# Seven block products in place of eight for half of an output projection, with half of z between them, on one Trainium2 core

## The chip, the cores and the metric

The kernel runs on one core of a Trainium2 chip. The metric is device time in microseconds, the median of several runs. Beside it one execution was profiled: its span runs from the first to the last instruction. The runs of the kernel before read 955.54, 956.37 and 956.94 us; the profiled span is 953.9 us. The profile gives no time around the span.

## The reference

One decoder layer on 512 tokens of width 1024, in float32:

```python
proj = x @ w_in
z, xbc, dt_raw, q, k, v, g = _split_cols(proj, IN_SIZES)
...                       # SSD scan of x|B|C gives y; retention of q, k, v gives yr
u = (y.reshape(bsz, seqlen, SSD_INNER) * jax.nn.silu(z.astype(f32)))    # then RMS norm -> y_ssd
yr = yr * gn_w.astype(f32) + gn_b.astype(f32)
y_ret = jax.nn.silu(g.astype(f32)) * yr
y_mix = jnp.concatenate([y_ssd, y_ret], axis=-1).astype(x.dtype)
return y_mix @ w_out      # 2048 x 1024; the lower 1024 rows are the retention half
```

After it come a layer norm, cross attention into 256 memory tokens, a second norm, a gated feed-forward of width 2752 and a third norm.

## The kernel before

Every dense product is done in three matmuls. A float32 operand is split into a part h (a cast to fp32r) and a rest l, and `mm3` (L156) adds h·h, h·l and l·h in a PSUM bank. Weights come as one stream of 157 groups of 128x1024 (`Stream`, L111): a DMA on SP's queue into one of three raw slots, a cast on ScalarE to `wh`, a subtraction on VectorE to `wl` (on GpSimd for the groups in `POOL_L`). Three groups are prepared ahead of the one in use, in rings of four.

TensorE's order is the order in which the code is written (`pin`, L96). The other engines' order comes from a list scheduler that takes, of what it thinks ready, what stands first in the code. A dense product is a generator. `feat` (L161) makes 128 features by 512 tokens out of one weight group, in four steps of six matmuls; `tok` (L172) makes four token tiles by 512 columns out of several groups, four steps of six matmuls a group, with the evacuation `done(t, b)` in the last group. `weave` (L198) runs a chain of dependent work and takes as many dense steps between its pieces as the chain yields.

The stages, in order:

- q, k, v (L267 to L366); the retention core (`retention`, L374) in four chunks of 128 tokens, woven into the x|B|C projection with 2 + 2 + 6 + 1 steps a chunk; its normalised outputs are transposed into `YT` after the six;
- the SSD (`ssd`, L520), four chunks woven into the eight gate products (one per retention head, `gate`, L608) and the first half of z (`z_gate`, L622). A gated head is split into `yret`, one cast and one subtraction of 128x512 each. In an SSD chunk `seg` (L541) makes decay factors on ScalarE, multiplies them on VectorE (L550), and `diag` (L553) uses them in the first products on them some steps later;
- the second half of z alone (L638); the z gate runs over ScalarE, VectorE and GpSimd (L623 to L632);
- four residual loads into `acc` on GpSimd's queue, kept in program order (L642);
- the retention half of the output projection: two `tok` products (column halves) of eight groups, added to `acc` by `into_acc` (L645). Woven into it, `ssd_out` (L669) transposes the SSD's output tile by tile after 4, 3, 3 and 3 steps and splits it;
- the SSD half (L716 to L727), the first norm, keys and values of the memory, attention, second norm, feed-forward, third norm.

`norm_t` (L703) transposes a normed token tile into `xT`, two splits of 128x512 a tile. Tiles lie in several sets of buffers: `s` (20), `acc` (4), `row` (2) and `x` (4 of double size).

## Time and profile before

| what | us |
| --- | --- |
| median of three runs (955.54 to 956.94) | 956.37 |
| span of the profiled execution | 953.9 |
| TensorE busy | 944.3 |
| VectorE busy | 563.6 |
| ScalarE busy | 340.9 |
| GpSimd busy | 140.0 |

Busy time is the time in which an engine works on an instruction; waiting for semaphores is not in it. The ends of matmuls are modelled and overlap, so 382 ns of one matmul is not the pace of many: the pace is read from a run of matmuls in the chain of waits. The mean granted TensorE clock was 0.998 of full speed.

### The profile page before, as it was taken

How to read it: one execution, taken by the hardware profiler on the slowest of the kernel's cores; microseconds unless marked ns; L12 is line 12 of the kernel's file. 1: busy time of each engine (PE TensorE's matmuls, PEld its weight loads, DVE VectorE, ACT ScalarE, POOL GpSimd, SP SyncE). 2: the span in 40 equal slices, each digit the busy share in tenths (PEclk: the TensorE clock that was granted, in tenths of full speed). 3: DMA queues.
4: the chain of work that ended last, by engine and by line, in shares of the span. 5: the costliest groups of instructions: out<-in, count | busy, mean ns of one | idle time of the engine just before them, and what ended most of it. 6: DMA issues, size and time to landing. Idle time of an engine off the chain costs nothing.

```text
span 953.9 us, 11550 instructions
## 1 busy us (share of the span) xinstructions
PE 944.3 (99%) x4607; PEld 776.5 (81%) x4607; DVE 563.6 (59%) x847; ACT 340.9 (36%) x487; POOL 140.0 (15%) x150
## 2 busy tenths in 40 slices
PE   9999999999999999999999999999999999999996
PEld 6788877788777888889888888988888888888874
DVE  5652566687765463448645668766535566336577
ACT  4122333345443431223533413544323443224420
POOL 1330110014252530065000006000000000000003
PEclk9999999999999999999999999999999999999999
DMA  8233211222211262425621112432322323323202
GB/s 296 87 115 103 67 45 67 67 89 67 67 45 67 89 221 88 154 89 176 221 88 47 67 66 89 136 108 88 98 101 89 111 89 95 103 89 110 89 22 89
DMA packets 26981, 95.24 MB, mean 100 GB/s; under 512 B 3120, under 2 KB 3632, under 8 KB 26928
## 3 DMA queue, kind: packets, MB, share of 16 engines
q1 hardware_dynamic: 25056, 88.09, 27.7%
q0 software_dynamic: 1728, 6.29, 1.9%
q8 instruction: 36, 0.59, 0.3%
q14 instruction: 17, 0.14, 0.1%
q10 hardware_dynamic: 144, 0.13, 0.0%
HBM read 92.41 MB, written 2.10 MB: 99 GB/s over the span
## 4 chain that ended last, share of the span: by engine, by line
PE 97%; DVE 1%; DMA 1%; SPq 0%; issue 0%; ACT 0%; DVEq 0%
PE b L104 95%; PE b L108 3%; DMA raw<-in_wst 1%; DVE acc L699 0%; DVE acc L692 0%; DVE x L153 0%; SPq L221 0%; DVE wl L128 0%; DVE acc L857 0%; DVE st L687 0%; ACT wh L126 0%; SPq L124 0%; DVEq L1073 0%; DVE st L688 0%
## 5 line engine op out<-in xcount | busy, mean ns | idle before, releaser
L104 PE MATMUL b<-x,wh 128*128 128x512 f32 (+1 forms) x1200 | 359.1, 382 | 0.5 <-DVE x L153 0.5
L128 DVE TENSOR_TENSOR wl<-raw,wh 128x1024 fp32r<-128x1024 f32 (+1 forms) x146 | 179.9, 1234 | 225.9 <-ACT wh L126 225.3
L126 ACT CAST wh<-raw 128x1024 fp32r<-128x1024 f32 (+1 forms) x157 | 164.8, 1050 | 311.5 <-PE b L104 275.1
L104 PEld LDWEIGHTS b<-x,wh 128*128 128x128 f32 x1200 | 218.2, 188 | 45.0 <-issue 4.2
L104 PE MATMUL b<-x,wl 128*128 128x512 f32 (+1 forms) x600 | 227.1, 378 | 0.0
L104 PE MATMUL b<-wh,s 128*128 128x512 f32 (+2 forms) x680 | 214.1, 391 | 0.0
L104 PE MATMUL b<-wh,x 128*128 128x512 f32 x512 | 163.2, 395 | 0.0
L104 PEld LDWEIGHTS b<-wh,s 128*128 128x128 f32 (+1 forms) x680 | 127.3, 188 | 30.7 <-issue 5.1
L104 PE MATMUL b<-wl,s 128*128 128x512 f32 (+1 forms) x340 | 131.5, 387 | 0.0
L104 PEld LDWEIGHTS b<-x,wl 128*128 128x128 f32 x600 | 112.9, 188 | 21.3
L104 PEld LDWEIGHTS b<-wh,x 128*128 128x128 f32 x512 | 96.0, 188 | 23.6 <-issue 2.2
L104 PE MATMUL b<-wl,x 128*128 128x512 f32 x256 | 99.9, 390 | 0.7 <-DVE wl L128 0.7
L104 PEld LDWEIGHTS b<-wl,s 128*128 128x128 f32 x340 | 63.9, 188 | 12.2
L257 POOL TENSOR_TENSOR st<-st,epst 128x1 f32<-128x1 f32 (+1 forms) x16 | 3.1, 192 | 479.6 <-DVE st L688 479.2
L894 DVE SCALAR_TENSOR_TENSOR t<-b,pr,t 128x511 f32<-128x511 f32 x86 | 64.1, 746 | 1.4
L104 PEld LDWEIGHTS b<-wl,x 128*128 128x128 f32 x256 | 48.1, 188 | 11.4 <-DVE wl L128 1.1
L128 POOL TENSOR_TENSOR wl<-raw,wh 128x1024 fp32r<-128x1024 f32 x12 | 34.8, 2916 | 68.5 <-ACT wh L126 68.5
L892 ACT ACTIVATE t<-b,cw,pr 128x512 f32<-128x512 f32 x43 | 33.3, 775 | 0.0
L908 ACT CAST s<-t 128x512 fp32r<-128x512 f32 (+1 forms) x22 | 13.6, 620 | 54.3 <-DVE t L906 54.3
L897 ACT ACTIVATE t<-t 128x512 f32<-128x512 f32 x21 | 13.3, 632 | 42.2 <-DVE t L895 42.2
L649 DVE TENSOR_TENSOR acc<-acc,b 128x512 f32<-128x512 f32 x24 | 15.8, 678 | 17.9 <-PE b L104 17.9
L104 PE MATMUL b<-s,wh 128*128 128x256 f32 x128 | 23.4, 285 | 0.0
(166 smaller groups left out, 856.3 us busy)
## 6 DMA issues: line engine op xcount, KB each, us to landing
raw<-in_wst SPq DMA_DIRECT2D x156, 512.0 KB, 3.3
row<-in_rows POOLq DMA_DIRECT2D x7, 512.0 KB, 6.2
acc<-in_xn POOLq DMA_DIRECT2D x4, 512.0 KB, 6.4
s<-in_xt SPq DMA_DIRECT2D x3, 512.0 KB, 7.7
out_y<-acc SPq DMA_DIRECT2D x3, 512.0 KB, 2.6
raw<-in_memt SPq DMA_DIRECT2D x2, 512.0 KB, 3.3
raw<-in_wst SPq DMA_DIRECT2D x2, 256.0 KB, 3.3
s<-in_xt SPq DMA_DIRECT2D x2, 256.0 KB, 4.3
```

The source lines that it names most:

```text
L104: pin(nc.tensor.matmul(o, lhsT=lhsT, rhs=rhs, start=start, stop=stop))
L108: pin(nc.tensor.transpose(o, i, ident[:p, :p]))
L126: copy(out=h[:, c], in_=r[:, c])
L128: sub_l(out=l[:, c], in0=r[:, c], in1=f(h[:, c]), op=sub)
L257: gtt(out=o, in0=v, in1=epst[:, :n], op=add)
L649: tt(out=a, in0=a, in1=b, op=add)
L892: nc.scalar.activation(out=c, in_=u, func=AF.Identity, bias=cw[0][:, i:i + 1], scale=ffp[:, i, 2:3])
L894: stt(out=c[:, d:], in0=u[:, :T - d], scalar=ffp[:, i, 2 - d:3 - d], in1=c[:, d:], op0=mult, op1=add)
L897: nc.scalar.activation(out=c, in_=c, func=AF.Silu)
L908: nc.scalar.copy(out=hd[:n, 0, :], in_=ca[:n, :])
```

## The change

The retention half of the output projection, 512 tokens x 1024 by 1024 x 1024, is cut in quarters on both sides and done in seven block products (Winograd's form of Strassen's scheme). `Sides` makes the sums of the left side in place in `YT`: with heads 2 and 3 it splits the first quarter, with heads 6 and 7 the second, and forms four combinations of 128x512 each time; the other five operands are split by `make` up to two products ahead. `Quarter` makes those of the right side: eight raw weight blocks are loaded four items further ahead than the ring, each load on SP's queue held until TensorE has reached that place in the program; item T2 has three combinations of 128x1024 on VectorE, T3 one, for each of two row blocks. Each product has two items of 12 matmuls. Products that share a PSUM bank pair are added there (`start` False), and after each product its sum is evacuated into `acc`.

The second half of z is no longer done alone: one of its four groups follows each of the first four products. The residual loads now stand in the program before it. The SSD's transposes wait for 51 steps. A retention chunk has 2 + 2 + 4 steps, and its outputs are transposed in the next chunk, after the scores. All large tiles come from one set of 37 buffers; `xT` is eight tiles instead of four, and `norm_t` makes four splits of 128x256. The descriptor area of DMAs issued by GpSimd is set to 4096 bytes. The same code can treat v and the down projection so, which `SEVEN` leaves off.

```diff
-NS = 20
-# columns of the constant array
+NS = 37
+SEVEN = ("ret",)
+RET_MIX = (1, 1, 1, 1, 0, 0, 0)
+AHEAD = 4
...
-    def slot(tag, shape, dt=F32, bufs=4):
-        return act.tile(shape, dt, tag=tag, name=nm(tag), bufs=bufs)
     def big(shape, dt=F32):
-        return slot("s", shape, dt, NS)
+        return act.tile(shape, dt, tag="s", name=nm("s"), bufs=NS)
...
+    class Quarters:
+        ORDER = ("11", "21", "T2", "T1", "T3", "22", "T4")
+        def __init__(self, n):
+            self.n, self.r = n, {}
+        def items(self):
+            return [[Quarter(self, what, k) for k in range(2)] for what in self.ORDER]
+    class Quarter:
+        PLACE = {"110": 0, "111": 1, "210": 2, "211": 3, "120": 4, "220": 5, "121": 6, "221": 7}
+        def __init__(self, of, what, k):
+            self.of, self.what, self.k = of, what, str(k)
+        def load(self):
+            for q in {"11": ("11",), "21": ("21",), "T2": ("12", "22")}.get(self.what, ()):
+                t = big([P, 1024])
+                d = nc.sync.dma_start(out=t, in_=wst[self.of.n + self.PLACE[q + self.k]])
+                tc.add_manual_dep(d.ins, last_pe[0].ins.name,
+                                  mybir.DependencyInfo(mybir.DependencyClass.Sync, mybir.DependencyReason.DATA),
+                                  reason="not before its time")
+                self.of.r[q + self.k] = t
+        def split(self):
+            r, k = self.of.r, self.k
+            b11, b12, b21, b22 = [r.get(q + k) for q in ("11", "12", "21", "22")]
+            src = {"11": b11, "21": b21, "T1": b11, "T3": b12, "22": b22, "T4": b21}.get(self.what)
+            if self.what == "T2":
+                src = raw_slot()
+                tt(out=b11, in0=b12, in1=b11, op=sub)
+                tt(out=src, in0=b22, in1=b11, op=sub)
+                tt(out=b21, in0=b21, in1=src, op=sub)
+            elif self.what == "T3":
+                tt(out=b12, in0=b22, in1=b12, op=sub)
+            h, l = pair()
+            nc.scalar.copy(out=h, in_=src)
+            tt(out=l, in0=src, in1=f(h), op=sub)
+            return h, l
...
+        def push(self, *args):
+            self.q.append(self.plan[self.n].split(*args))
             self.n += 1
         def get(self, n):
-            while self.n < self.total and self.n <= self.i + RING - 1:
+            while self.m < len(self.plan) and self.m <= self.i + RING - 1 + AHEAD:
+                self.plan[self.m].load()
+                self.m += 1
...
+    def mixed(products, others, after):
+        out, others = [], list(others)
+        for p, n in zip(products, after):
+            out += p
+            out += others[:n]
+            others = others[n:]
+        return out + others
+    plan = groups(0, 8)
+    plan += mixed(Quarters(8).items(), groups(16, 4), V_MIX) + groups(20, 8) if "v" in SEVEN else groups(8, 20)
+    plan += groups(28, 12)
+    plan += mixed(Quarters(44).items(), groups(40, 4), RET_MIX) if "ret" in SEVEN else groups(40, 12)
...
+    def seven(side, done):
+        bk = {}
+        order = ((1, "11", "u", True), (2, "12", "b", True), (6, "S2", "u", False), (5, "S1", "c", True),
+                 (7, "S3", "u", False), (3, "S4", "c", False), (4, "22", "u", False))
+        def product(i):
+            m, a, where, start = order[i]
+            if start:
+                bk[where] = [bank() for _ in range(2)]
+            for n in range(i, min(i + 3, 7)):
+                side.make(order[n][1])
+            for kp in range(2):
+                wh, wl = W.get(2)
+                for t in range(2):
+                    for j in range(2):
+                        k = 2 * kp + j
+                        mm3(bk[where][t], side(a, k, t), (wh[:, j, :], wl[:, j, :]), start and k == 0, k == 3, not start)
+                    if kp == 1:
+                        done(m, t, bk[where][t])
+                    yield
+        return [product(i) for i in range(7)]
+    def behind(products, others, after):
+        for p, n in zip(products, after):
+            yield from p
+            for _ in range(n):
+                yield from next(others)
+    GOES = {1: (0, 0, True), 2: (0, 0, False), 6: (0, 1, True), 5: (2, 1, True), 7: (2, 1, False),
+            3: (0, 1, False), 4: (2, 0, True)}
+    class Sides:
+        def __init__(self, raws, have=None):
+            self.raws, self.got = raws, dict(have or {})
+        def pair(self, name):
+            if name not in self.got:
+                self.got[name] = big([P, 4, 256], F32R), big([P, 4, 256], F32R)
+            return self.got[name]
+        def split(self, name, p, src):
+            h, l = self.pair(name)
+            c = slice(2 * p, 2 * p + 2)
+            nc.scalar.copy(out=h[:, c, :], in_=src)
+            tt(out=l[:, c, :], in0=src, in1=f(h[:, c, :]), op=sub)
+        def view(self, i, j, p):
+            return self.raws[2 * j + p][:, :, 256 * i:256 * i + 256]
+        def ready(self, p):
+            if p < 2:
+                if p == 0:
+                    self.s1 = None
+                    self.own = "11" not in self.got
+                if self.own:
+                    self.split("11", p, self.view(0, 0, p))
+                return
+            p -= 2
+            if self.s1 is None:
+                self.s1 = big([P, 4, 256])
+            s1 = self.s1[:, 2 * p:2 * p + 2, :]
+            a11, a12, a21, a22 = [self.view(i, j, p) for i in range(2) for j in range(2)]
+            if self.own:
+                self.split("12", p, a12)
+            tt(out=s1, in0=a21, in1=a22, op=add)
+            tt(out=a21, in0=a11, in1=a21, op=sub)
+            tt(out=a11, in0=s1, in1=a11, op=sub)
+            tt(out=a12, in0=a12, in1=a11, op=sub)
+        def make(self, name):
+            if name in self.got:
+                return
+            for p in range(2):
+                self.split(name, p, {"S1": lambda: self.s1[:, 2 * p:2 * p + 2, :], "S2": lambda: self.view(0, 0, p),
+                                     "S3": lambda: self.view(1, 0, p), "S4": lambda: self.view(0, 1, p),
+                                     "22": lambda: self.view(1, 1, p)}[name]())
+        def __call__(self, a, k, t):
+            g = self.got[a]
+            if callable(g):
+                return g(k, t)
+            return g[0][:, k, t * P:(t + 1) * P], g[1][:, k, t * P:(t + 1) * P]
...
+            if c > 0:
+                yn_transposes(c - 1, yn)
             yield 2
...
-            yield 6
...
-            yield 1
...
+            yield 4
+        yn_transposes(NT - 1, yn)
...
+            if "ret" in SEVEN:
+                stt(out=y, in0=sg, scalar=0.5, in1=y, op0=mult, op1=mult)
+                if j in (2, 3, 6, 7):
+                    ret_side.ready(j // 4 * 2 + j % 2)
+                return
...
+    ret_side = Sides([YT[0], YT[2], YT[1], YT[3]])
...
-    drain(tok(x_lhs, all8, NT, z_gate(1)))
-    acc = [slot("acc", [P, 1024], F32) for _ in range(NT)]
+    z_rest = tok(x_lhs, all8, NT, z_gate(1))
+    if "ret" not in SEVEN:
+        drain(z_rest)
+    acc = [big([P, 1024]) for _ in range(NT)]
...
+    def acc_quarter(scale=None):
+        def done(m, t, b):
+            t0, n, first = GOES[m]
+            into_acc(n, scale if first else None)(t0 + t, b)
+        return done
...
-        yield 4
+        yield 51 if "ret" in SEVEN else 4
         for t in range(NT):
-            ys = slot("x", [P, 2, 8, P], F32R)
-            to_features(X[t], lambda g: ys[:, 0, 4 * g:4 * g + 4, :], lambda g: ys[:, 1, 4 * g:4 * g + 4, :])
-            yssd.append(ys)
-            yield 3
-    dense = seq(*[tok(tok2(yret), all8, NT, into_acc(n, ALPHA)) for n in range(2)])
+            yssd.append((big([P, 8, P], F32R), big([P, 8, P], F32R)))
+            to_features(X[t], split_into(*yssd[t]))
+            yield 4 if "ret" in SEVEN else 3
+    if "ret" in SEVEN:
+        dense = behind(seven(ret_side, acc_quarter(ALPHA)), pieces(z_rest, NT), RET_MIX)
+    else:
+        dense = seq(*[tok(tok2(yret), all8, NT, into_acc(n, ALPHA)) for n in range(2)])
...
     def norm_t(t):
-        to_features(acc[t], lambda g: xT[g][:, :, t * P:(t + 1) * P], lambda g: xT[2 + g][:, :, t * P:(t + 1) * P])
+        def put(g, b):
+            for i in range(2):
+                h, l = [x[:, :, t * P:(t + 1) * P] for x in xT[2 * g + i]]
+                split_ps(b[:, 2 * i:2 * i + 2, :], h, l)
+        to_features(acc[t], put)
...
+    heads = np.concatenate([np.arange(P) + 1024 + P * h for h in (0, 2, 1, 3, 4, 6, 5, 7)])
+    g.append(_quarters(wo, heads, every) if "ret" in SEVEN else _tok(wo, slice(1024, 2048), every))
...
-    nc = bacc.Bacc("TRN2", target_bir_lowering=False, num_devices=1)
+    nc = bacc.Bacc("TRN2", target_bir_lowering=False, num_devices=1, dynamic_dma_scratch_size=4096)
```

## Rows read from the trace of the kernel before

**Rows 1.** The page: busy us (share) xinstructions of each engine.

```profile
PE 944.3 (99%) x4607; PEld 776.5 (81%) x4607; DVE 563.6 (59%) x847; ACT 340.9 (36%) x487; POOL 140.0 (15%) x150
```

**Rows 2.** The waits of TensorE: line waited for, us in total, times, longest.

```profile
PE b L104 <- DVE wl L128: 0.7, 1, 0.7
PE b L104 <- DVE x L153: 0.5, 1, 0.5
```

**Rows 3.** Chain in order of time, 300 to 430 us: start, us, what.

```profile
336.96 0.87 PE b L108 x8
337.83 4.10 PE b L104 x18
341.93 0.87 PE b L108 x8
342.81 4.13 PE b L104 x18
```

**Rows 4.** Windows: stretch, length, busy us (x) per engine, clock, DMA share, GB/s.

```profile
197.00:217.00 20.00, 20.00 (x102) 16.78 (x101) 16.85 (x27) 9.97 (x18) 0.00 (x0) 1.00 0.32 105
309.40:378.90 69.50, 69.50 (x324) 57.87 (x323) 33.64 (x42) 25.19 (x43) 22.69 (x37) 1.00 0.40 136
105.00:199.00 94.00, 94.00 (x535) 75.75 (x534) 61.19 (x153) 33.88 (x56) 12.66 (x20) 1.00 0.20 65
```

**Rows 5.** VectorE by line, 309.4 to 378.9 us: busy, mean ns, idle before.

```profile
L128 DVE TENSOR_TENSOR wl<-raw,wh 128x1024 fp32r<-128x1024 f32 x12 | 14.6, 1221 | 18.8 <-ACT wh L126 18.8
L632 DVE SCALAR_TENSOR_TENSOR s<-s,st,row 128x512 f32<-128x512 f32 x8 | 6.1, 763 | 11.4 <-POOL st L631 11.4
L651 DVE SCALAR_TENSOR_TENSOR acc<-acc,b 128x512 f32<-128x512 f32 x8 | 5.4, 684 | 2.2 <-PE b L104 2.2
```

**Rows 6.** Five lines' own views: duration ns min/median/max, first and last start.

```profile
L512 DVE TENSOR_TENSOR acc<-s,dt x4: 1216/1220/2308, 216.0 to 278.1; 128x1024 f32<-128x1024 f32 x4
...
L537 DVE TENSOR_TENSOR t<-b,cs x4: 411/424/424, 219.0 to 289.7; 128x256 f32<-128x256 f32 x4
...
L126 ACT CAST wh<-raw x157: 620/1055/1072, 5.6 to 921.2; 128x1024 fp32r<-128x1024 f32 x156, 128x512 fp32r<-128x512 f32 x1
...
L616 ACT CAST s<-t x8: 602/620/621, 215.8 to 276.7; 128x512 fp32r<-128x512 f32 x8
...
L617 DVE TENSOR_TENSOR s<-t,s x8: 677/688/1026, 217.2 to 277.5; 128x512 fp32r<-128x512 f32 x8
```

**Rows 7.** VectorE in order of time, 255 to 290 us.

```profile
266.64 1.19 DVE L614 SCALAR_TENSOR_TENSOR t<-t,s 128x512 f32<-128x512 f32 x1
...
269.68 1.96 DVE L550 TENSOR_TENSOR t<-t,t 128x512 f32<-128x512 f32 x2 [0.32 <-ACT t L549]
```

**Rows 8.** TensorE in order of time, 262 to 292 us.

```profile
271.19 1.08 PE L104 MATMUL b<-acc,t 128*128 128x64 f32 x8
```

**Rows 9.** The page's DMA issues: KB each, us to landing.

```profile
raw<-in_wst SPq DMA_DIRECT2D x156, 512.0 KB, 3.3
```

**Rows 10.** GpSimd in order of time, 280 to 350 us.

```profile
320.50 0.22 POOL L631 TENSOR_SCALAR st<-st 128x1 f32<-128x1 f32 x1
...
341.81 0.22 POOL L631 TENSOR_SCALAR st<-st 128x1 f32<-128x1 f32 x1
342.02 2.20 POOL L642 DMA_DIRECT2D acc<-in_xn  x4
```

**Rows 11.** The view of L642, the residual loads.

```profile
DMA to landing us min/median/max: 3.6/6.4/10.0
```

**Rows 12.** The view of L626, the z gate's multiplication.

```profile
L626 POOL TENSOR_TENSOR s<-s,t x8: 1280/1293/2203, 307.8 to 337.0; 128x512 f32<-128x512 f32 x8
```

More of the change, by code (lines that the diff above doesn't have):

```diff
@@ L189, in drain, with pieces @@
+    def pieces(gen, n):
+        while True:
+            yield islice(gen, n)
     def drain(*gens):
@@ L282, in rotary, with v_quarter @@
         return done
+    def v_quarter(m, t, b):
+        t0, n, first = GOES[m]
+        v = V[t0 + t][:, n * 512:(n + 1) * 512]
+        if first:
+            nc.scalar.copy(out=v, in_=b)
+        else:
+            tt(out=v, in0=v, in1=b, op=add)
     def v_done(n):
@@ L372, in tile_layer, with yn_transposes @@
     YT = [big([P, 2, T]) for _ in range(4)]
+    def yn_transposes(c, yn):
+        for g in range(2):
+            b = bank()
+            for j in range(4):
+                transpose(b[:, j * P:(j + 1) * P], yn[g][:, j * P:(j + 1) * P])
+            for j in range(2):
+                nc.scalar.copy(out=YT[2 * g + j][:, :, c * P:(c + 1) * P],
+                               in_=b[:, 256 * j:256 * j + 256].rearrange("p (j t) -> p j t", j=2))
     def retention():
+        yn = None
         for c in range(NT):
@@ L486, in xbc @@
     def xbc():
-        for g in range(2):
-            yield from feat(xk, T, conv_silu(8 + g, BT[:, g, :]))
-        for g in range(2):
-            yield from feat(xk, T, conv_silu(10 + g, CT[:, g, :]))
+        if not BC:
+            for tile_ in bc_tiles():
+                yield from tile_
         b_transposes()
@@ L752, in v_mem @@
         return done
-    xT = [slot("x", [P, 4, T], F32R) for _ in range(4)]
+    xT = new_x()
     def first_norm():
@@ L860, in tile_layer @@
     gs = [W.get(2) for _ in range(4)]
-    xT = [slot("x", [P, 4, T], F32R) for _ in range(4)]
+    xT = new_x()
     for t in range(NT):
@@ L932, in tile_layer @@
     drain(hg)
[L933 to L939 removed]
+    up = (feat(xk, T, ff_done(i)) for i in range(4, NFF))
+    if "down" in SEVEN:
+        drain(*islice(up, 14))
+        drain(behind(seven(hid_side[0], acc_quarter(ALPHA)), up, UP_MIX[0]))
+        drain(*islice(up, 2))
+        drain(behind(seven(hid_side[1], acc_quarter()), up, UP_MIX[1]))
+        drain(*up)
+    else:
+        for n in range(2):
+            drain(*islice(up, 16 if n else 12))
+            for m in range(2):
+                drain(tok(tok2(hid), range(8 * n, 8 * n + 8), NT, into_acc(m, None if n else ALPHA)))
+        drain(*up)
+    for n in range(2):
+        drain(tok(tok2(hid), [16, 17], NT, into_acc(n)))
     gs = [W.get(2) for _ in range(4)]
```

187 lines of the change are left out of this document (114 added, 73 removed).

## The prediction

> **What bounds the kernel now.** I read the busy table first. TensorE is busy 944.3 of 953.9 us, VectorE 563.6 [rows 1]. The list of TensorE's waits comes next: behind its matmuls stand two waits of 0.7 and 0.5 us and nothing else after the start [rows 2]. So the kernel is one queue of matmuls, and an edit changes the time in two ways only: it takes matmuls out of the queue, or it makes the queue wait. The chain of waits gives the price of a matmul: 18 products of 512 columns in 4.13 us, 0.229 us each [rows 3].
>
> The profiled span is 953.9 us; the three runs of before read 955.54 to 956.94. I take 2.5 us around the span, so a span of X goes with X + 2.5, and a change of the span is carried to the median of 956.37 unchanged.
>
> The stage in question is found in the same chain. The first SSD transposes stand at 336.96 [rows 3], and the code puts four steps of six products before them, 24 x 0.229 = 5.5 us, so the retention half begins at 331.4. Before it lies the second half of z, 96 products or 22.0 us, from 309.4. The retention half is 192 products, 44.0 us, with 4 x 0.87 us of transposes: it ends at 378.9. In these 69.5 us TensorE is busy for 69.50, VectorE 33.64, ScalarE 25.19, GpSimd 22.69 [rows 4].
>
> **The matmuls.** Two column halves of 8 row blocks by 4 token tiles by 3 partial products are 192 matmuls. Seven quarter products of 4 row blocks by 2 token tiles by 3 are 168. Of 24 matmuls fewer, 24 x 0.229 = **5.5 us** come off the queue. Nothing else in the change touches the count of products or transposes, so this is also the most it can gain, up to the 1.2 us of waits in [rows 2]. The stage would last 64.0 us.
>
> **What VectorE gets for it in the stage.** Weight items go from 12 to 18, each with a subtraction of 1.22 us [rows 5]: 6 more, 7.3 us. Eight combinations of whole weight blocks, 128x1024 from SBUF, have no row of their own; the nearest, a product of 128x1024, takes 1.22 us, at most 2.31 [rows 6]: 9.8 us, at most 18.5. Five left operands are split inside the stage in two pieces each: 10 x 0.69 us [rows 6] = 6.9. Evacuations go from 8 to 14: 6 x 0.68 [rows 5] = 4.1. Together 28.1 us, so VectorE has 33.6 + 28.1 = 61.7 us of work in 64.0, 96%. ScalarE gets 6 casts of 1.05 us and 10 of 0.62 [rows 6], 12.5 us: 37.7 of 64.0, no bound.
>
> Does TensorE wait for this? From below: nothing. The 84% stretch at 197 to 217 us has VectorE at 16.85 of 20 us and TensorE without a gap [rows 4]; the eight combinations can run ahead, since their blocks are loaded seven items before their place; the weights of the next stage (about three of 1.22 us) and most SSD splits are due after it. From above: VectorE keeps its idle time in front of the z norm (half of 11.4 us, which waits for GpSimd) and of the evacuations (2.2 us) [rows 5]; then it needs 61.7 + 5.7 + 2.2 = 69.6 us, and 5.6 us go back, the whole gain. I take **1.5 us**, nearer to the stretch with the row.
>
> **The transposes behind the stage.** The new first step count, 51, exceeds the 44 steps that there are (28 of the products, 16 of z). So all 32 transposes run bare after the last product, 3.5 us, and the first SSD product of tile 0 needs only the first of eight splits. A step of six products takes 6 x 0.229 = 1.38 us; the seventh split is due 3.5 + 3 x 1.38 = 7.6 us after the transposes start; two last evacuations and seven splits are 9 x 0.68 = 6.1 us (a split by its row in [rows 6]). Cover 1.5 us; one weight subtraction in between (1.22) fits. Cost 0; if VectorE comes late by x us, x - 1.5.
>
> **The gate.** The split of the eight gated heads falls to four, but at heads 6 and 7 four combinations follow (4 x 0.69 us, by the split's row [rows 6]). Head 6 matters: its gating ends at 267.8, the decay products of the SSD run at 269.68 (two of them, 1.96 us), and the first SSD product on them starts at 271.19 [rows 7, 8]. That is about 0.5 us of slack against 2.8 us of new work with an earlier place in the program. Bounds: 0, if the order puts the decay products first, and 2.3 us. I take **1.2 us**, the middle, since nothing shows the order. Head 7 has idle time behind it.
>
> **Retention steps.** Eight steps a chunk instead of eleven take 12 x 1.38 = 16.6 us of filling out of the woven part. Its window has VectorE at 61.19 of 94.0 us [rows 4]; if all of that work stayed in the shorter window it would fill 61.2 / 77.4 = 79%, under the 84% that TensorE passed without a gap. The normalised outputs are now transposed one chunk later, behind 4 + 2 steps and the next scores, no earlier than the six of now. Cost 0, gain 0, as TensorE doesn't wait there. If the cover went, each of four chunks could lose a step, 1.4 us.
>
> **One set of buffers.** The layer-norm splits become four of 128x256 instead of two of 128x512 per tile: 4 x 0.42 [rows 6] against 2 x 0.68 us on VectorE, 0.3 us later for the last, but earlier for the first, and the 0.5 us wait in [rows 2] is for such a first one. 0, within 0.3 either way. Quarter loads sit in SP's queue until TensorE reaches their place, and the plain loads queue behind them; those are still three groups (16 us) early, against 3.3 us of landing [rows 9], 1.05 of cast and 1.22 of subtraction. 0; without this lead, 5.6 us once.
>
> The residual rows are moved: they are now issued before the second half of z. In the trace the four loads start at 342.02, right behind GpSimd's last z operation [rows 10], so they will start behind the first half's, at 320.7 [rows 10]. They land 6.4 us later (3.6 to 10.0) [rows 11], at 327 to 331. The first product's bank is reused at 309.4 + 22.0 = 331.4, after an evacuation of 0.68 us that needs two of them. 0, and up to 1 us.
>
> This change also shrinks the area for the descriptors of GpSimd's loads to 4 KB. The Trainium skill ("SBUF — State Buffer", section "SBUF size: 192, 224, or 256?") gives that area as 16 KiB and says nothing of a smaller one; no row here shows one.
>
> **Sum.** -5.5 + 1.5 + 1.2 = -2.8 us: a span of 951.1, a median of **953.6 us**.
>
> **Rivals.**
> *The queue hides everything*: no wait is added. For it: no gap at 84%, and combinations that can run early. Against: 0.5 us of slack at head 6. 956.4 - 5.5 = 950.9.
>
> *VectorE becomes the bound of the stage*: 96% is a mean, and VectorE serves its queue in order. 3.5 to 7 us go back; with 5.6 from above and 1.2 of the gate, 957.7 us; around 956 if half of the stage's idle is filled. For it: the idle time in front of the z norm. Against: the deadlines are spread, and 3 to 4 us of the work may slip past the stage. A second road leads here. The multiplications of the z gate on GpSimd take 1.28 us or 2.20 [rows 12], the longer when VectorE works beside them, and the 128x1024 product of VectorE 1.22 or 2.31 [rows 6]. If each of the eight multiplications around the stage held VectorE for 1.28 us, 10.2 us would join the 61.7: 71.9 against 64.0, 7.9 lost, 958.8. Against: the stage's subtractions average 1.22 us [rows 5], so there GpSimd paid.
> The Trainium skill ("SBUF — State Buffer", section "SBUF: two separate sides") states it as an exclusive lock between a GpSimd operation and a VectorE one with two SBUF inputs; the two pairs of durations agree, and all combinations and splits added here are of that kind.
>
> *Slower: the residual rows come late.* The loads go one after the other instead of together. Two of them at the longest landing seen, 2 x 10.0 from 320.7, put the second at 340.7; with 0.68 of evacuation the bank is free at 341.4, where TensorE wants it at 332.8: it stands 8.6 us, with VectorE's queue held behind that evacuation. 956.4 - 5.5 + 8.6 = 959.5. It is slower than before once the second lands after 337.6. For it: the smaller area; against: the trace issues four in 2.20 us without a wait [rows 10].
>
> *The product count isn't what the text says*: excluded by counting; only a wait can hide it.
>
> **Chances.** Forecast 0.42, nothing lost 0.20, VectorE bound 0.24, rows late 0.14. Differences under 0.2% (1.9 us) can't be told from none here. Faster (under 954.5): 0.20 + 0.39 of the forecast = 0.59. Within: 0.03 of it and most of the bound case, 0.25. Slower (over 958.3): late rows and the worst of the bound case, 0.16. The range 950.3 to 958.6 leaves out the late rows and some of that; the forecast's own is 952 to 954.6.
>
> **What would show it.** 168 products in the retention half. Right: TensorE's waits stay under 3 us, and the z and retention stage lasts 64 to 66 us. Gate wrong: no gap before the SSD products of the third chunk, or over 2.5 us. Bound case: VectorE over 95% of the stage and TensorE waiting for weight parts. Late rows: VectorE idle before the first evacuation, released by the residual loads. The forecast fails if the waits of that stage exceed 3 us, or if none at all is seen.

## The result, and the profile after

The changed kernel reads 965.37 us (963.92 to 966.11), the one before 956.5 beside it: 1.0091 times the time, 95% interval 1.0079 to 1.0103. It is slower by about 9 us where 2.8 us of gain were forecast, and the time lies above the range.

The page's busy table of the changed kernel answers to [rows 1]:

```profile
PE 944.4 (98%) x4583; PEld 775.7 (81%) x4583; DVE 596.3 (62%) x897; ACT 351.3 (36%) x515; POOL 142.9 (15%) x150
```

TensorE has the 24 matmuls fewer that were counted (4607 to 4583), and yet the same busy time: some of those that are left are slower. The list of TensorE's waits, to be read beside [rows 2]:

```profile
PE b L108 <- DVE s L245: 3.3, 3, 1.7
PE b L108 <- DVE wl L186: 2.4, 2, 1.2
PE b L108 <- DVE s L877: 2.3, 1, 2.3
PE b L108 <- ACT wh L185: 1.2, 1, 1.2
PE b L241 <- DVE t L238: 1.2, 1, 1.2
PE b L108 <- DVE s L413: 0.6, 1, 0.6
PE b L108 <- DVE t L770: 0.4, 1, 0.4
```

L185 and L186 are the cast and the subtraction of a quarter item, L877 the evacuation into `acc`, L244 and L245 cast and subtraction of `split_ps`. Where before had 0.7 and 0.5 us of waits behind its matmuls, there are now three groups: 5.95 us in the z and retention stage (L186 twice, L185, L877), 3.3 us at the two norms (L245: 1.68 in front of a product of the memory's keys, 1.37 and 0.27 in front of the feed-forward's first ones), and 1.0 in single places (0.4 of it the gate's, L770, at 270.62). The wait on L238 is the start's.

The windows of the same kernel (columns as in [rows 4]) show what a wait does beyond its own length:

```profile
308.90:382.90 74.00, 68.05 (x297) 54.99 (x297) 57.13 (x67) 34.90 (x56) 24.10 (x38) 0.95 0.33 114
...
322.00:330.00 8.00, 8.00 (x36) 6.35 (x35) 7.33 (x9) 3.69 (x7) 2.68 (x6) 1.00 0.72 262
339.00:342.50 3.50, 3.50 (x10) 2.69 (x10) 3.50 (x6) 2.65 (x4) 0.00 (x0) 0.51 0.76 227
373.00:376.50 3.50, 3.50 (x10) 2.73 (x9) 3.50 (x5) 0.00 (x0) 0.00 (x0) 0.53 0.44 177
448.30:452.00 3.70, 3.68 (x30) 3.69 (x31) 3.67 (x7) 3.70 (x9) 2.07 (x3) 1.00 0.53 177
595.00:598.20 3.20, 3.20 (x17) 3.20 (x16) 3.10 (x4) 0.15 (x1) 3.20 (x2) 0.51 0.70 219
```

In three stretches of 3.2 to 3.5 us TensorE is busy all the time at a granted clock of 0.51 to 0.53, the level of 1.2 GHz. Each stands behind waits: two of 1.21 us within 3 us, one of 2.31, one of 1.37 and one of 0.27. Each costs about half of itself: 3.5 x 0.49 + 3.5 x 0.47 = 3.4 us in the stage, 3.2 x 0.49 = 1.6 at the start of the feed-forward. Behind the single waits of 1.22 (322 to 330) and 1.68 us (448.3) the clock stayed at 1.00.

Nor does the clock fall behind such waits each time. The runs described below have some of the same ones at 1.00: in order, behind 2.34 us (e2_norm_512), behind 1.22 and 1.21 within 3 us (f3_casts_first), behind 1.37 and 0.28 (e4_no_chain):

```profile
374.10:378.00 3.90, 3.87 (x17) 3.23 (x18) 3.90 (x6) 0.83 (x1) 0.00 (x0) 1.00 0.61 194
...
339.50:346.00 6.50, 6.46 (x28) 5.37 (x29) 6.50 (x8) 4.16 (x6) 0.00 (x0) 1.00 0.55 161
...
585.00:591.00 6.00, 5.97 (x50) 5.97 (x51) 5.52 (x7) 1.69 (x4) 5.92 (x5) 1.00 0.69 221
```

What decides it isn't shown here. A difference between two runs can therefore hold 1.6 to 1.7 us for each such slow stretch that came in one and not in the other.

So the loss has two parts, read from where the same work starts in both traces: the keys of the memory start 4.6 us later (422.03 and 426.61), although 5.5 us of products are gone ahead of them, and the rest is added at the two norms (+6.5 behind the first, +9.3 behind the second, +9.3 at the end).

**In the stage.** VectorE's lines between 308.9 and 382.9 us, beside [rows 5]:

```profile
L186 DVE TENSOR_TENSOR wl<-s,wh 128x1024 fp32r<-128x1024 f32 x10 | 12.2, 1219 | 2.3 <-ACT wh L185 2.3
L139 DVE TENSOR_TENSOR wl<-raw,wh 128x1024 fp32r<-128x1024 f32 x7 | 8.5, 1220 | 1.0 <-ACT wh L138 1.0
L858 DVE SCALAR_TENSOR_TENSOR s<-s,st,s 128x512 f32<-128x512 f32 x8 | 8.1, 1013 | 11.6 <-POOL st L857 10.5 <-ACT s L335 1.1
```

The 18.8 us that VectorE idled in front of weight subtractions have been filled. The 11.4 us in front of the z norm's scaling (L632, now L858) have not: they are 11.6. In order of time, GpSimd, ScalarE, VectorE and TensorE around the longest wait:

```profile
364.76 2.20 POOL L852 TENSOR_TENSOR s<-s,t 128x512 f32<-128x512 f32 x1 [1.47 <-DVE t L823]
...
366.99 0.63 ACT L854 ACTIVATE t<-s 128x512 f32<-128x512 f32 x1 [3.13 <-POOL s L852]
...
368.23 0.77 DVE L858 SCALAR_TENSOR_TENSOR s<-s,st,s 128x512 f32<-128x512 f32 x1 [2.42 <-POOL st L857]
369.78 0.75 DVE L858 SCALAR_TENSOR_TENSOR s<-s,st,s 128x512 f32<-128x512 f32 x1 [0.77 <-POOL st L857]
370.44 1.22 DVE L186 TENSOR_TENSOR wl<-s,wh 128x1024 fp32r<-128x1024 f32 x1
371.58 1.28 DVE L877 TENSOR_TENSOR s<-s,b 128x512 f32<-128x512 f32 x2
...
372.41 0.47 PE L108 MATMUL b<-wh,s 128*128 128x512 f32 x1 [2.31 <-DVE s L877]
...
373.57 0.63 PE L108 MATMUL b<-wl,s 128*128 128x512 f32 x1
373.99 1.05 PE L108 MATMUL b<-wh,s 128*128 128x512 f32 x2
374.85 0.63 PE L108 MATMUL b<-wl,s 128*128 128x512 f32 x1
```

GpSimd's multiplication takes 2.20 us. ScalarE stands 3.13 us for it with its square, and VectorE 2.42 and 0.77 us for GpSimd's small operations. Behind them in VectorE's queue stand a weight subtraction and the evacuation that frees TensorE's bank, so TensorE waits 2.31 us, and three products then take 1.28 us (373.57 to 374.85) instead of 0.69. Before, the same idle times (1.91, 2.43 and 0.77 us at 335 to 342) had nothing urgent behind them; the last two of VectorE's trace before:

```profile
340.52 0.77 DVE L632 SCALAR_TENSOR_TENSOR s<-s,st,row 128x512 f32<-128x512 f32 x1 [2.43 <-POOL st L631]
342.06 0.75 DVE L632 SCALAR_TENSOR_TENSOR s<-s,st,row 128x512 f32<-128x512 f32 x1 [0.77 <-POOL st L631]
342.73 1.22 DVE L128 TENSOR_TENSOR wl<-raw,wh 128x1024 fp32r<-128x1024 f32 x1
```

**At the norms.** The same view around the first norm's splits, ScalarE, VectorE, TensorE:

```profile
442.05 0.65 ACT L244 CAST s<-b 128x256 fp32r<-128x256 f32 x2 [4.77 <-DVE s L245]
...
443.13 0.41 DVE L245 TENSOR_TENSOR s<-b,s 128x256 fp32r<-128x256 f32 x1
443.65 3.42 DVE L938 SCALAR_TENSOR_TENSOR s<-s,st,s 128x1024 f32<-128x1024 f32 x1
446.99 3.68 DVE L245 TENSOR_TENSOR s<-b,s 128x256 fp32r<-128x256 f32 x8
...
448.32 0.50 PE L108 MATMUL b<-s,wh 128*128 128x256 f32 x2 [1.68 <-DVE s L245]
```

The second cast of a half tile waits for VectorE's subtraction of the first (ACT behind DVE L245), so a half tile goes between the two engines twice, and each time it joins VectorE's queue behind a norm operation of up to 3.42 us.

### The profile page after: what moved, and what is told of

It reads as the page before. It is cut to its first block, busy times and chain, and to the rows that moved or that the text cites. A ratio compares the mean times of both kernels' runs of the same rounds, so it can differ in the third digit from the quotient of the medians.

```text
span 963.2 us, 11593 instructions
## 1 busy us (share of the span) xinstructions
PE 944.4 (98%) x4583; PEld 775.7 (81%) x4583; DVE 596.3 (62%) x897; ACT 351.3 (36%) x515; POOL 142.9 (15%) x150
## 4 chain that ended last, share of the span: by engine, by line
PE 87%; DVE 6%; POOL 3%; issue 2%; ACT 1%; DMA 0%; DVEq 0%; SPq 0%; POOLq 0%
PE b L108 85%; PE b L112 2%; POOL s L852 1%; DVE s L938 1%; DVE s L931 1%; DVE wl L139 1%; DVE wl L186 1%; POOL st L856 0%; DVE s L877 0%; DMA s<-in_xt 0%; DVE t L823 0%; POOL s L802 0%; DVE st L926 0%; ACT wh L138 0%; POOL st L449 0%
## 5 line engine op out<-in xcount | busy, mean ns | idle before, releaser
L108 PE MATMUL b<-s,wh 128*128 128x512 f32 (+1 forms) x1328 | 383.6, 374 | 3.3 <-DVE s L245 3.3
L108 PE MATMUL b<-wh,s 128*128 128x512 f32 (+1 forms) x1176 | 374.1, 394 | 4.1 <-DVE s L877 2.3
L108 PEld LDWEIGHTS b<-s,wh 128*128 128x128 f32 x1328 | 239.5, 189 | 48.0 <-issue 4.4
L108 PEld LDWEIGHTS b<-wh,s 128*128 128x128 f32 (+1 forms) x1176 | 221.8, 189 | 59.1 <-issue 7.2
L108 PE MATMUL b<-s,wl 128*128 128x512 f32 (+1 forms) x664 | 245.8, 370 | 0.0
L108 PE MATMUL b<-wl,s 128*128 128x512 f32 (+1 forms) x588 | 229.9, 391 | 2.4 <-DVE wl L186 2.4
L108 PEld LDWEIGHTS b<-s,wl 128*128 128x128 f32 x664 | 125.8, 189 | 21.5
L108 PEld LDWEIGHTS b<-wl,s 128*128 128x128 f32 x588 | 111.2, 189 | 25.8 <-DVE wl L186 3.5
L244 ACT CAST s<-b 128x512 fp32r<-128x512 f32 (+1 forms) x64 | 28.8, 488 | 53.9 <-PE b L112 22.3
L245 DVE TENSOR_TENSOR s<-b,s 128x512 fp32r<-128x512 f32 (+1 forms) x64 | 33.2, 548 | 14.9 <-ACT s L244 14.7
L108 PE MATMUL b<-s,t 128*128 128x64 f32 (+2 forms) x240 | 32.6, 281 | 0.4 <-DVE t L770 0.4
L877 DVE TENSOR_TENSOR s<-s,b 128x512 f32<-128x512 f32 x30 | 19.7, 678 | 17.9 <-PE b L108 17.9
```

The source lines that it names most:

```text
L108: pin(nc.tensor.matmul(o, lhsT=lhsT, rhs=rhs, start=start, stop=stop, skip_group_check=more))
L244: nc.scalar.copy(out=h, in_=src)
L245: tt(out=l, in0=src, in1=f(h), op=sub)
L877: tt(out=a, in0=a, in1=b, op=add)
```

## The experiments

Times are medians; ratios, with 95% intervals, are to the kernel before on the same chip. It reads 956.1 to 956.6 us on the chips of these runs, so a difference between two runs can hold half a microsecond of that.

**The norm splits.** Three runs: the rest of the change without the seven products; 128x512 splits with `x` in four double tiles of their own (29 buffers stay in the one set); and both casts ahead of both subtractions.

```diff
# e1_rest_only
-SEVEN = ("ret",)
+SEVEN = ()
# e2_norm_512
-            for i in range(2):
-                h, l = [x[:, :, t * P:(t + 1) * P] for x in xT[2 * g + i]]
-                split_ps(b[:, 2 * i:2 * i + 2, :], h, l)
+            split_ps(b, xT[g][:, :, t * P:(t + 1) * P], xT[2 + g][:, :, t * P:(t + 1) * P])
# f3_casts_first
-                split_ps(b[:, 2 * i:2 * i + 2, :], h, l)
+                nc.scalar.copy(out=xT[2 * g + i][0][:, :, t * P:(t + 1) * P], in_=b[:, 2 * i:2 * i + 2, :])
+            for i in range(2):
+                h, l = [x[:, :, t * P:(t + 1) * P] for x in xT[2 * g + i]]
+                tt(out=l, in0=b[:, 2 * i:2 * i + 2, :], in1=f(h), op=sub)
```

> The changed kernel with the eight-product form (v, output and down projection all plain): only the retention steps, the one set of buffers, the 128x256 norm splits and the small descriptor area are left of the change. Theory 'the norm splits cost some 5 us': TensorE's waits near 448 and 593 us stay, the start gains 0.8, so 956.5 - 0.8 + 2.0 + 2.8 = 960.5. Rival 'all of the loss belongs to the seven products': 955.7 to 956.5.

> The changed kernel with x in four tiles of double size in a set of their own (29 buffers left in the other) and the norm's output split as before, one cast and one subtraction of 128x512 a half tile. Theory 'the norm splits': the waits at the first norm and at the feed-forward's start go, 965.4 - 4.7 = 960.7. Rival 'buffers or the shifted order': no change, 964 to 966.

> The changed kernel with one edit: in the norm's split of 128x256 pieces both casts of a half tile come first, then both subtractions. Theory 'the second cast waits for the first subtraction, so a half tile passes twice between ScalarE and VectorE, and each pass queues behind the norm's long operations': the waits at 448 and 593 us go and the run comes to 961, as with one split of 128x512. Rival 'the smaller pieces themselves, or the tiles of x': 964 to 966.

Measured: e1_rest_only 959.1 us, 1.003 (1.0019 to 1.0042); e2_norm_512 961.13, 1.0054 (1.0039 to 1.0069); f3_casts_first 962.62, 1.0065 (1.005 to 1.008). Without the seven products the kernel is still 3 us slower, and of the three groups of waits just the norms' 3.3 us (L245) are left. TensorE's waits in e2_norm_512, and one line of the list of f3_casts_first, where L948 is the norm splits' subtraction:

```profile
PE b L108 <- DVE wl L186: 2.4, 2, 1.2
PE b L108 <- DVE s L880: 2.3, 1, 2.3
PE b L108 <- ACT wh L185: 1.2, 1, 1.2
...
PE b L108 <- DVE x L245: 0.5, 1, 0.5
```

```profile
PE b L108 <- DVE s L948: 2.5, 2, 1.3
```

The double tiles take the norm's waits away, all but the 0.5 us of [rows 2], leave the stage's as they were, and are worth 965.4 - 961.1 = 4.2 us (waits 3.3 - 0.5, slow stretch 1.6: 4.4). Casts first gives 2.75 of these 4.2 us, but not as expected: the norms' waits don't go, they shrink from 3.3 to 2.5 us. The second handover is thus 0.8 us of waits. The rest is the clock: the profiled run of f3_casts_first lacks the slow stretch at the feed-forward (1.6 us), and one of 1.7 in the z and retention stage, which the edit doesn't touch. These 4.1 us, less the 1.0 by which this execution was later before the stage (the gate's products start at 271.63 against 270.62), are the 3.1 between the two profiled runs. What keeps the 2.5 us of waits is a place in VectorE's queue. At the first norm two of a tile's four subtractions still stand behind the norm's operation of 3.43 us (443.12) and start at 446.47; in e2_norm_512 both of a tile's two start ahead of that operation, at 442.02 and 443.76. At the second an evacuation (591.22) stands between two of the pieces.

**The stage: amount or order?** Three runs on the changed kernel: the weight combinations left out (the products then use raw blocks); the RMS norm of the z gate left out (multiplication on VectorE, a constant scale); and all of z's second half ahead of the seven products.

```diff
# e3_no_combos
-                src = raw_slot()
-                tt(out=b11, in0=b12, in1=b11, op=sub)
-                tt(out=src, in0=b22, in1=b11, op=sub)
-                tt(out=b21, in0=b21, in1=src, op=sub)
+                src = b22
...
-                tt(out=b12, in0=b22, in1=b12, op=sub)
# e4_no_chain
-            gtt(out=Xh, in0=Xh, in1=sz, op=mult)
...
-            stt(out=Xh, in0=Xh, scalar=rs, in1=norm_w[...], op0=mult, op1=mult)
+            tt(out=Xh, in0=Xh, in1=sz, op=mult)
+            stt(out=Xh, in0=Xh, scalar=0.5, in1=norm_w[...], op0=mult, op1=mult)
# f5_z_first
-    plan += mixed(Quarters(44).items(), groups(40, 4), RET_MIX)
+    plan += groups(40, 4) + mixed(Quarters(44).items(), [], RET_MIX)
...
+    drain(z_rest)
```

> The changed kernel without the eight combinations of weight blocks on VectorE (the products use the plain blocks: the sums of the weights are left out). 9.8 us of VectorE work leave the stage. Theory 'too much work on VectorE': all four waits of the stage go with their slow clock, 965.4 - 9 = 956 to 957. Rival 'the z gate's chain over GpSimd stops VectorE's and ScalarE's queues': the waits at 321 and 372 stay, 960 to 963.

> The changed kernel with the z gate's RMS norm left out (no square on ScalarE, no three small operations on GpSimd, a constant in place of the factor) and its multiplication on VectorE instead of GpSimd: VectorE gets 8 x 0.68 us more work and no longer waits for GpSimd. Theory 'the z gate's chain stops the queues': the waits at 321 and 372 go, 956 to 960. Rival 'too much work': no better, 964 to 968.

> The changed kernel with the second half of z done alone ahead of the seven products (the residual loads stay ahead of both). Theory 'the z gate's chain': the chain falls into 22 us in which few weights are due, only a part of it meets the combinations, 957 to 961. Rival 'z between the products is the cover that VectorE needs': 43 us of its work against 38.5 us of products, 966 to 972.

Measured: e3_no_combos 960.5 us, 1.0044 (1.0027 to 1.0061); e4_no_chain 953.54, 0.9973 (0.9961 to 0.9985); f5_z_first 963.52, 1.0074 (1.0059 to 1.0089). Leaving out eight VectorE operations of 1.22 us gives 4.9 us: the wait at 321 goes, the two near 337 shrink to 0.6 and 0.8, the wait of 2.3 us at the z gate's chain stays, and no slow stretch is left in the stage. Leaving out the chain gives 11.9 us, with more work for VectorE (1.6 of it is the slow stretch at the feed-forward, which did not come in this run). The window of e4_no_chain over the stage:

```profile
308.90:380.90 72.00, 72.00 (x336) 60.19 (x335) 64.38 (x83) 33.44 (x44) 1.06 (x3) 1.00 0.35 122
```

VectorE is busy for 64.38 of 72.00 us, more than the 57.13 of 74.00 above, and TensorE has no gap. So it is not the amount by itself: less work behind the idle times cures a part of the waits, and no idle times in front of the work cure all of them. Moving z ahead of the products gains 1.9 us, less than was expected: the wait of 2.31 goes, and those on L186 and L185 grow to 3.7 and 1.5 us.

**Which part of the chain?** f1_mult_on_dve: 128x512 splits as in e2_norm_512, and the z gate's multiplication on VectorE, the rest of the chain as it was. f1p_scale_on_pool has the final scaling as two multiplications on GpSimd besides, and the last group of z's second half one product earlier.

```diff
# f1_mult_on_dve (on e2_norm_512)
-            gtt(out=Xh, in0=Xh, in1=sz, op=mult)
+            tt(out=Xh, in0=Xh, in1=sz, op=mult)
# f1p_scale_on_pool (on f1)
-            stt(out=Xh, in0=Xh, scalar=rs, in1=norm_w[...], op0=mult, op1=mult)
+            gtt(out=Xh, in0=Xh, in1=norm_w[...], op=mult)
+            gtt(out=Xh, in0=Xh, in1=rs.to_broadcast([P, 512]), op=mult)
-RET_MIX = (1, 1, 1, 1, 0, 0, 0)
+RET_MIX = (1, 1, 2, 0, 0, 0, 0)
```

> The kernel with the norm's split of 128x512 (961.1 us) and, beside it, the z gate's multiplication moved from GpSimd to VectorE; the square on ScalarE and the three small operations on GpSimd stay. Theory 'the z gate's chain over GpSimd stops the queues': the long member of the chain (1.28 to 2.20 us, one after another) is gone, and of the 12 us of waits and slow clock half or more go: 950 to 956. Rival 'any wait for GpSimd in VectorE's order is enough': 959 to 962, as the three small operations are still waited for.

> As the one before, and the gate's last scaling (factor and row of weights) done by two multiplications on GpSimd instead of one operation on VectorE, with the groups of z after products 1, 2 and 3 (one, one, two) to give GpSimd time. VectorE then waits for GpSimd nowhere in the stage. Theory 'only the wait in VectorE's queue matters': 949 to 952. Rival 'GpSimd becomes late': some 20 us more of its work, the SSD's transposes wait for the last tiles, 955 to 960.

Measured: 953.29 us, 0.9969 (0.9957 to 0.9982), and 964.52, 1.0085 (1.007 to 1.01). The first beats the kernel before, 7.8 us under e2_norm_512. The second gives it all back, by another road that neither expectation had (949 to 952, or 955 to 960). First GpSimd in order of time, then the waits of 318 to 345 us, both of f1p_scale_on_pool:

```profile
330.01 1.04 POOL L862 TENSOR_TENSOR s<-s,st 128x512 f32<-128x512 f32 x1
331.00 2.20 POOL L874 DMA_DIRECT2D s<-in_xn  x4
```

```profile
DVE s L883 <- DMA s<-in_xn: 12.5, 2, 11.8
...
PE b L108 <- DVE s L883: 4.0, 1, 4.0
```

The residual loads are issued only at 331.00, behind GpSimd's queue; VectorE stands 11.8 us for them in front of an evacuation, and TensorE 4.0. That is the prediction's "residual rows come late", brought about by GpSimd's load and not by the descriptor area: in the changed kernel itself four loads are issued by 324.2 and land in

```profile
DMA to landing us min/median/max: 3.6/5.4/7.2
```

**Controls.** The multiplication on VectorE in the kernel before; no chain and 128x512 splits together; the first operation of each T2 on GpSimd; and f1_mult_on_dve without the seven products.

```diff
# g1_before_mult (on the kernel before)
-            gtt(out=Xh, in0=Xh, in1=sz, op=mult)
+            tt(out=Xh, in0=Xh, in1=sz, op=mult)
# g2_chain_and_norm: e4_no_chain and e2_norm_512 together
# g3_t2_on_pool (on f1)
-                tt(out=b11, in0=b12, in1=b11, op=sub)
+                gtt(out=b11, in0=b12, in1=b11, op=sub)
# g4_mended_no_seven (on f1)
-SEVEN = ("ret",)
+SEVEN = ()
```

> The kernel before with one edit: the multiplication of the z gate goes from GpSimd to VectorE (8 operations of 128x512). Theory (the z gate's chain costs nothing while TensorE never waits for it, so the edit that gave about 8 us in the changed kernel gives nothing here): 956.3 us, within 0.2 per cent of before. Rival (the multiplication on GpSimd costs time by itself, by slowing VectorE, in any kernel with this stage): 953 us or less.

> The changed kernel without the chain of the z gate (no RMS norm of the gated z; its multiplication on VectorE, the scaling by a constant) and with the layer-norm splits of 128x512. Theory (the two causes are separate and together are all that the change lost): 953.5 - 4.2 = 949.3 us, no TensorE wait over 0.6 us in the z and retention stage, none in front of the FFN beyond the 0.5 us that before had. Rival (they share a cause, such as the load on VectorE, so that their gains don't add): 951.5 to 953.5. Rival (something else of the change, such as retention steps, gives time by itself): under 949.

> The changed kernel with the z gate's multiplication on VectorE and 128x512 splits (953.3 us) and one more edit: of the weight combinations the first of each T2 block (2 of 8, 128x1024) goes to GpSimd, which is idle there. Theory (the wait of 1.2 us near 336, behind a T2 part, is VectorE's queue being full of combinations; the operation on GpSimd is early enough): that wait goes, with the slow clock behind it, 951 to 952.3 us. Rival (a 128x1024 product on GpSimd takes 2 to 3 us and the two after it on VectorE wait for it, so VectorE's queue stands): wait of 2 us or more, 954 us or above.

> The changed kernel with the z gate's multiplication on VectorE and 128x512 splits, but with the retention half of the projection in its eight row blocks again (192 products). Theory (with both causes mended the rest of the change is worth nothing either way): 956.3 us, within 0.15 per cent of before, no waits beyond those of before; the seven products are then worth 3.0 us of their 5.5 in the mended kernel. Rival (the gain over before comes from the rest of the change and not from the seven products): 953 us.

Measured: g1_before_mult 955.83 us, 0.9995 (0.9986 to 1.0003); g2_chain_and_norm 950.3, 0.9939 (0.9927 to 0.9951); g3_t2_on_pool 958.33, 1.0016 (1.0007 to 1.0024); g4_mended_no_seven 955.13, 0.999 (0.9982 to 0.9999). The edit that is worth 7.8 us in the changed kernel is worth nothing measurable before: there the chain has nothing behind it. With both causes gone the kernel gains 956.3 - 950.3 = 6.0 us, the whole 5.5 within the intervals. The window of g2_chain_and_norm over the shorter stage:

```profile
308.00:377.00 69.00, 69.00 (x322) 57.67 (x322) 64.09 (x82) 32.39 (x43) 1.55 (x3) 1.00 0.36 129
```

VectorE at 93%, and TensorE without a gap. g3_t2_on_pool is 5.0 us slower than f1. GpSimd's operation takes 2.40 us and is done at 326.6, in time. But VectorE's own combination beside it is held (the line is VectorE's in g3_t2_on_pool; in f1 the same operation takes 1.22 us):

```profile
323.93 3.81 DVE L180 TENSOR_TENSOR raw<-s,s 128x1024 f32<-128x1024 f32 x1
```

These 2.6 us, and a changed order behind them, bring VectorE to the second T2 part's operation (L180) at 335.87, against 331.74 in f1, and TensorE waits 1.88 and 1.24 us and runs at a mean clock of 0.83 from 335 to 345 us. The rival's time was right, and so was VectorE standing for GpSimd, though beside its operation and not for its result. How much each of the two gives was not separated. g4_mended_no_seven is 1 us better than before, so the seven products are worth 955.1 - 953.3 = 1.8 us in f1, less than the 3.0 expected.

**Order alone.** All runs so far that cured the stage also took the multiplication off GpSimd. h3_norm_later leaves each operation on its engine and changes its place: the square and the small operations come behind the next block product, the scaling behind the one after. h2_later_and_dve does so with the multiplication on VectorE, h5_fewer_ahead also makes left operands two products ahead instead of three.

```diff
# h3_norm_later (on e2_norm_512); h2_later_and_dve: the same on f1
+    def after_pe(o):                    # not before TensorE has reached this place
+        tc.add_manual_dep(o.ins, last_pe[0].ins.name, ..., reason="later")
+    def tail(sz, Xh, ss, rs, n):
+        a = nc.scalar.activation(out=sz, in_=Xh, func=AF.Square, accum_out=ss)
...
+        after_pe(a)
+        t2_.append(lambda: after_pe(stt(out=Xh, in0=Xh, scalar=rs, in1=norm_w[...], op0=mult, op1=mult)))
...
             gtt(out=Xh, in0=Xh, in1=sz, op=mult)
...
+            t1.append(lambda: tail(sz, Xh, ss, rs, n))
...
             into_acc(n, scale if first else None)(t0 + t, b)
+            if t == 1:
+                later()                 # what t2_ holds, then what t1 holds
# h5_fewer_ahead (on h2)
-            for n in range(i, min(i + 3, 7)):
+            for n in range(i, min(i + 2, 7)):
```

> The changed kernel with 128x512 splits (961.1 us), all operations of the z gate on the engines where the change has them, the multiplication on GpSimd too; only the order is changed: the square and the three small operations are issued behind the next block product's last matmul, the scaling on VectorE behind the one after, so that neither queue stands for GpSimd. Theory (the loss is VectorE and ScalarE standing in their order for the GpSimd chain, not the work of GpSimd or its speed): no idle time of VectorE in front of the scaling, no TensorE wait over 1.3 us, 952 to 954.5 us. Rival (GpSimd's 128x512 multiplication slows VectorE beside it, whatever the order): 957 us or above. Rival (VectorE simply has too much work in the stage): 957 us or above, with VectorE busy to 95 per cent and TensorE waiting for weight parts.

> The same later order with the z gate's multiplication on VectorE. Theory: the idle time is gone already, so the multiplication's place matters little: within 1 us of the run with it on GpSimd, 951.5 to 954. Rival (VectorE's load decides): slower than it by the 5.5 us of multiplications that VectorE gets. Rival (GpSimd's use of the memory port decides): faster than it by 3 us or more.

> As the run before, and left operands are made two products ahead instead of three, so that fewer 128x512 splits stand in VectorE's queue among the combinations near 336 us. Theory (what is left against 950.3 is the one wait of 1.2 us near 336 behind the second T2 part, a matter of order in VectorE's queue): that wait shrinks or goes, 950.5 to 952 us. Rival (the splits then come too late themselves): a wait for a left operand's part, 953 us or more.

Measured: h3_norm_later 951.3 us, 0.9943 (0.993 to 0.9955); h2_later_and_dve 950.54, 0.9936 (0.9922 to 0.9949); h5_fewer_ahead 950.91, 0.994 (0.9928 to 0.9952). The three can't be told apart, and all beat both kernels; the first two come 0.7 and 1.0 us under what was expected. The wait near 336 that h5_fewer_ahead was for is gone in h2_later_and_dve already, so that run decides nothing. Of h3_norm_later the list of TensorE's waits, the stage's window, and VectorE's and GpSimd's lines in it:

```profile
...
PE b L108 <- DVE wl L139: 0.7, 1, 0.7
PE b L108 <- DVE x L245: 0.5, 1, 0.5
PE b L108 <- DVE x L416: 0.5, 1, 0.5
PE b L108 <- DVE t L773: 0.4, 1, 0.4
```

```profile
308.00:377.00 69.00, 68.94 (x321) 57.25 (x320) 62.14 (x73) 37.08 (x59) 27.97 (x38) 1.00 0.35 122
```

```profile
L186 DVE TENSOR_TENSOR wl<-s,wh 128x1024 fp32r<-128x1024 f32 x10 | 14.2, 1426 | 3.1 <-ACT wh L185 3.1
...
L864 DVE SCALAR_TENSOR_TENSOR s<-s,st,s 128x512 f32<-128x512 f32 x8 | 5.5, 745 | 0.0
...
L183 DVE TENSOR_TENSOR s<-s,s 128x1024 f32<-128x1024 f32 x2 | 3.5, 1760 | 0.0
```

```profile
L878 POOL TENSOR_TENSOR s<-s,t 128x512 f32<-128x512 f32 x8 | 14.1, 1784 | 27.9 <-DVE t L826 27.9
```

The scaling (L864) has no idle time in front of it, where there were 11.6 us. GpSimd's multiplications are no shorter (1.78 us in the mean), and VectorE's subtractions are lengthened (1426 ns against 1219), but none of TensorE's waits in the list lies in the stage (they are the start's, the gate's and the feed-forward's). 961.1 - 951.3 = 9.8 us of order alone; leaving the chain out (961.1 - 950.3, g2_chain_and_norm) gives 10.8, not clearly more. By the ratios, which take out the chips, these are 10.6 and 11.0.

## Why the prediction was wrong

The sum as it came out: 956.4 - 5.5 of products + 0.4 at the gate = 951.3, which is h3_norm_later; + 9.8 for the z gate's chain in the stage = 961.1, e2_norm_512; + 4.2 for the norm splits = 965.4. Only the first line is a test, since 9.8 and 4.2 are themselves differences of these runs. The trace of the changed kernel has 5.95 + 3.4 = 9.35 us of waits and slow clock for the one and 2.8 + 1.6 = 4.4 for the other.

**The step that failed first: "Does TensorE wait for this?", 1.5 us.** It measured 9.8. The step compared VectorE's work with the stage's length, 61.7 of 64.0 us, and took the stretch of [rows 4] at 84% without a gap as the nearest row. The amount turned out harmless where no idle time stood in the queue, even at 93% (g2_chain_and_norm). What decided was in its own upper bound, the idle time in front of the z norm of [rows 5], but read as a share of VectorE's time. It is a place in a queue that runs in order: whatever stands behind that scaling is as late as GpSimd is. Before, weight subtractions three groups ahead stood there; now it is a quarter item's subtraction that is due at once, the parts of T2 and the evacuation that frees a bank pair, for which TensorE stands. And the waits can have a price beyond their length that no term had: some 3.4 of the 9.8 us are TensorE at 0.51 to 0.53 of its clock behind them. The rows before showed the clock at 1.00 only, behind waits of 0.7 us and less.

**The second: "One set of buffers", 0 within 0.3 us.** It measured 4.2. Four pieces were priced by their durations, 4 x 0.42 against 2 x 0.68, and the first was to be earlier. Their durations differ by just these 0.3 us a tile. What counts is where they stand in VectorE's queue, which holds norm operations of up to 3.42 us: at the first norm, of four pieces a tile two stand behind such an operation, of two none does. These places, with the smaller pieces as such, are 2.0 of the 2.8 us of waits (f3_casts_first still has 2.5, e2_norm_512 0.5); that it is the places is read from the traces, not tested alone. The other 0.8 us is a handover: with four pieces a half tile goes from ScalarE to VectorE and back twice, and the second cast waits for the first subtraction. The remaining 1.6 us is the slow stretch. Between e4_no_chain and g2_chain_and_norm, neither of which has a slow stretch, the splits cost 953.5 - 950.3 = 3.2.

In the handover the two engines read different halves of one PSUM bank. The Trainium skill ("Advanced Engine Details and Errata", section "Bank Collisions") has a rule that the prediction did not weigh: ScalarE and VectorE cannot access one bank in the same cycle. The waits of the trace (4.77 and 3.52 us of ScalarE on L245) agree with an order kept for that reason; no run here put the halves into two banks.

**VectorE as the bound** was the rival nearest to what happened, with the right place, but a wrong reason and 957.7 or 958.8 us. The sign that it gave, VectorE over 95% of the stage, is not seen (57.13 of 74.00 us). Its second road, GpSimd holding VectorE's operations, happens and costs nothing in h3_norm_later: there the T3 combinations take 1760 ns in the mean against 1216 in the changed kernel, and TensorE does not wait. The Trainium skill ("SBUF — State Buffer", section "SBUF: two separate sides") says that a GpSimd operation and a VectorE one with two SBUF inputs shut each other out; the lengthened rows of both engines agree, most plainly the 3.81 us of g3_t2_on_pool, and the time of h3_norm_later shows that this was not the bound.

**Right:** 24 products fewer at 0.229 us (g2_chain_and_norm and h3_norm_later gain 6.0 and 5.3 us); the retention steps at nothing (that stage is 113.5 us before and 113.3 after); the transposes behind the stage and the quarter loads on SP's queue at nothing (no wait of TensorE names them); the residual loads and the 4 KB area at nothing (above). **The gate** was the right place and too dear: 0.43 us at 270.62 instead of 1.2. What it said would show a failure, waits of over 3 us in that stage, is what the page shows: 5.95.

**Open:** h3_norm_later and h2_later_and_dve differ by 0.8 us, less than their intervals, so whether GpSimd or VectorE is the better place isn't settled. What decides whether TensorE's clock falls behind a wait of 1 to 2.5 us isn't shown. Why ScalarE's second cast waits for the first subtraction is argued, not shown. Why the seven products are worth only 1.8 us in f1 isn't fully shown: its waits at 336 and 366 us are 1.22 and 0.59.

## What to carry to other kernels

An engine's idle time in front of an instruction that waits for a slower engine is not room for new work: it is a stretch in which everything queued behind stands. Before urgent work is added to a queue, look in the timeline for such waits and move the waiting instruction behind the urgent ones; here that alone was worth 9.8 us, against 5.5 us of matmuls saved. And price a split into smaller pieces by where each piece will stand in the queues of the engines that it passes, not by the pieces' durations.

## What the runs showed of the hardware

- The price of a short wait of TensorE need not be its length. In the changed kernel the granted clock was 0.51 to 0.53 for 3.2 to 3.5 us behind waits of 1.2 us twice within 3 us, of 2.3, and of 1.37 and 0.27, and three products of 512 columns took 1.28 us instead of 0.69; behind single waits of 1.22 and 1.68 us it stayed at 1.00. In other runs it also stayed at 1.00 behind 2.34 us (e2_norm_512), behind 1.22 and 1.21 (f3_casts_first) and behind 1.37 and 0.28 (e4_no_chain).
- VectorE can be busy for 64.09 of 69.00 us while TensorE, which it feeds, has no gap (g2_chain_and_norm).
- A subtraction of 128x1024 on VectorE took 3.81 us instead of 1.22 beside one of 2.40 us on GpSimd (g3_t2_on_pool).
